# Hybrid diffusion layers on one core: in the first layer, tokens are normalised and transposed ahead of their modulation, which then goes by two blocks at a time

## The chip, the cores and the metric

The kernel runs on one NeuronCore of one Trainium2 chip. The metric is the device time of one execution in microseconds (us). Engines: TensorE (PE), VectorE (DVE), ScalarE (ACT), GpSimd (POOL), SyncE (SP, which here only issues DMAs).

## What is computed

Two layers over 512 latent and 256 context tokens of width 1024. Each layer starts with a normalisation whose result is scaled and shifted by columns computed from a condition vector; only this start matters here:

```python
shift, scale, gate = split(silu(c) @ w_mod[l] + b_mod[l], 3)      # c_ctx for context tokens
h = rmsnorm(x, norm_gain[l]) * (1 + scale) + shift
za, zb, zh, zf, zg = split(h @ w_in[l], SPLIT_IDX)                # projections of four mixers and gates
# four mixers, merged by gates sigmoid(h @ w_merge) and projected by w_out
x = x + gate * merge_branches(h, (ya, yb, yh, yf), zg, w_up[l], w_merge[l], w_out[l])
```

All is float32. Projections are done as three matmuls in a rounded format (high x high, high x low, low x high), so every operand is split into a high and a low part.

## The kernel before, in words

The kernel records its instructions in program order, and a planner of its own (`Program.order`, line 255) writes the final order of each engine, by assumed costs, ranks and free buffers. What runs on the chip is that fixed order: each engine takes its instructions one after another and waits by semaphores. SBUF tiles of 768 columns come from one pool of 31 slots (`slot`, line 371); PSUM has three 512-wide tiles (`psg`), two 1024-wide ones (`psw`) and one more (`pst`). All instructions are recorded through one helper, so every row of the profile has line 345, and rows are told apart by tiles.

Tokens are kept transposed, as features on partitions: `h_hi` and `h_lo` hold eight blocks of 128 features by 768 tokens (latent 0 to 511, context 512 to 767). A projection (`gemm_a`, line 583) goes through the eight blocks with 24 matmuls; `mm3` (line 572) lets the planner cut between groups of `ATOM` = 4 blocks. The first is `hg_gates` (line 1166): two outputs of 128 features, each over 384 and 384 tokens. Weights come by SP in pieces of 512 KB (`Weights`, line 484: tile `wraw`), and are split by ScalarE (`wh`) and VectorE (`wl`).

The opening of layer 0 is `first_modulation` (line 632) with `loads` (line 1503). Four loads of 2 MB of modulation weights (scale and shift of feature blocks 0 to 3, then of 4 to 7), each in eight DMAs, alternate with the x tokens, half of them after the first and half after the second. For each load, eight matmuls against the condition (`spread`, tile `cst`) give rows, ScalarE copies them, four small matmuls turn them into columns (`psg<-kc,mrow`). `Norm.square` (line 712) makes the sums of squares on ScalarE, `Norm.scale` (line 717) a reciprocal root in a chain of 13 small VectorE operations and a diagonal matrix from it; `Norm.place` (line 729) multiplies each token tile by that matrix, which transposes and normalises at once, scales and shifts on the way out of PSUM and splits. Half of the blocks is placed after two of the four loads, the other half at the end. `modulation` (line 662) does the same columns for layer 1 later, 256 at a time.

Of the kernel before, what the change touches and what calls it, by code (L numbers as in the profile page):

```python
# [21 lines left out]
P = 128  # L22
# [327 lines left out]
def tile_hybrid_mixers(ctx, tc, io, out, dump=None):  # L350
# [221 lines left out]
    def mm3(ps, pairs):  # L572
        n = len(pairs)
        nc.ahead = -BEHIND
        for k, (sh, sl, mh, ml) in enumerate(pairs):
            if k % ATOM == 0:
                nc.cut()
# [5 lines left out]
    def gemm_a(wh, wl, cs, n0, n1):  # L583
        ps = psg()[:, 0:n1 - n0]
        mm3(ps, [(wh[k][:, cs], wl[k][:, cs], hi_t[:, k, n0:n1], lo_t[:, k, n0:n1]) for k in range(8)])
        return ps
# [45 lines left out]
    def first_modulation(loads):  # L632
# [3 lines left out]
        for g in range(2):  # L636
            ks = slice(4 * g, 4 * g + 4)
            for a in (1, 0):
                nc.ahead = AHEAD
                w = []  # L640
                for k in range(8):
                    w.append(slot([P, 512]))
                    nc.sync.dma_start(w[k], io["w_mod0"][g, a, :, 512 * k:512 * (k + 1)])
                loads()
                ps = psg()
                for r in range(4):
                    nc.cut()
                    spread(ps, lambda k: w[k], (2 * r, 2 * r + 1))
                rows = sp.tile([P, 512], F32, tag="mth", bufs=2, name=nm("mrow"))
                act(rows, ps)  # L650
                pc = psg()[:, 0:8]
                for b in range(4):
                    mm(pc[:, 2 * b:2 * b + 2], rows[:, P * b:P * (b + 1)], csel)
                nc.ahead = 0
                bm = cols[:, CO_BM + 8 * a + 4 * g:CO_BM + 8 * a + 4 * g + 4]
                tt(tmp[:, a, ks], pc.rearrange("p (k w) -> p k w", w=2), bm.unsqueeze(2).to_broadcast([P, 4, 2]), ALU.add)
            ng = cols[:, CO_NG + 4 * g:CO_NG + 4 * g + 4]
            stt(mc[:, 0, ks], tmp[:, 1, ks], 1.0, ng.unsqueeze(2).to_broadcast([P, 4, 2]), ALU.add, ALU.mult)
            nc.vector.tensor_copy(mc[:, 1, ks], tmp[:, 0, ks])
            yield mc  # L660

    def modulation(l):
# [4 lines left out]
        def columns(j, rows):  # L667
            ps = psg()[:, 0:4]
            for b in range(2):
                mm(ps[:, 2 * b:2 * b + 2], rows[:, P * b:P * (b + 1)], csel)  # L670
# [3 lines left out]
        for j in range(8):  # L674
            rows = mod_rows(fetched.pop(("mod", j)))
            unit_done(2.0)
            if last is not None:
                columns(*last)
# [1022 lines left out]
```

## Time and profile before

| | us |
|---|---|
| median of 3 runs (1528.56 to 1533.97) | 1529.69 |
| the profiled execution | 1535.81 |
| its span in the profile | 1534.0 |
| TensorE busy | 1479.5 |
| VectorE busy | 941.7 |
| ScalarE busy | 633.8 |

The page shows one profiled execution: busy times, the span in 40 slices, DMA queues, the chain of work that ended last, and the costliest groups. The trace behind it can be asked for a stretch, an engine or a tile. A busy TensorE is not one at its peak: matmuls overlap, so the spacing of their starts says more than the length of one. [...]

### The profile page before, as it was taken

What the parts mean: (1) busy time and instruction counts of PE and PEld (TensorE: products, weight loads), DVE (VectorE), ACT (ScalarE), POOL (GpSimd) and SP (SyncE); (2) the same over time, 40 slices, a digit from 0 to 9 for tenths busy, and PEclk for the clock granted to TensorE, in tenths of its full rate; (3) what the DMA queues carried; (4) which work ended last, traced back from release to release, by engine and by line L of the source; (5) the groups of instructions that cost most, each with busy time, mean ns of one, the idle gap of its engine ahead of it and who ended that gap; (6) DMA issues with size and microseconds to landing.
All of it is one profiled execution on the core that took longest, in us unless ns stands there. A gap on an engine that the chain in (4) does not pass through costs nothing.

```text
span 1534.0 us, 25450 instructions
## 1 busy us (share of the span) xinstructions
PE 1479.5 (96%) x10052; PEld 1345.8 (88%) x10052; DVE 941.7 (61%) x2048; ACT 633.8 (41%) x1416; POOL 107.3 (7%) x207
## 2 busy tenths in 40 slices
PE   6899999999999998899999999999999999999999
PEld 2799989889999998889999998898987889888788
DVE  3596788667663355552444467978966864674544
ACT  3534354466532243441322244445445643552321
POOL 0000000410000000100000110000041000110000
PEclk8999999999999999899999999999999999999999
DMA  9211001523321124253221422111153222445332
GB/s 344 82 56 56 32 29 56 121 62 96 124 86 56 56 76 133 61 190 103 77 85 62 125 98 75 57 45 55 50 151 99 87 81 71 129 127 187 110 109 74
DMA packets 50280, 144.76 MB, mean 94 GB/s; under 512 B 7473, under 2 KB 9521, under 8 KB 50161
## 3 DMA queue, kind: packets, MB, share of 16 engines
q1 hardware_dynamic: 38016, 112.21, 22.5%
q0 software_dynamic: 12144, 30.93, 8.0%
q8 instruction: 79, 1.29, 0.3%
q14 instruction: 41, 0.33, 0.1%
HBM read 123.98 MB, written 4.19 MB: 84 GB/s over the span
## 4 chain that ended last, share of the span: by engine, by line
PE 85%; DVE 5%; ACT 5%; issue 2%; DMA 2%; SPq 0%; POOL 0%; ACTq 0%; DVEq 0%; POOLq 0%
PE psg L345 71%; PE psw L345 10%; PE pst L345 4%; ACT u L345 3%; DVE u L345 3%; DVE sm L345 1%; ACT wh L345 1%; DMA u<-in_w_mod_dram 1%; DVE wl L345 1%; DMA u<-u 0%; ACT mth L345 0%; DMA u<-in_rpb_dram 0%; SPq L345 0%; DVE psw L345 0%; ACT sq L345 0%
## 5 line engine op out<-in xcount | busy, mean ns | idle before, releaser
L345 PE MATMUL psg<-h_hi,wh 128*128 128x384 f32 (+2 forms) x1248 | 450.7, 361 | 5.4 <-ACT mth L345 2.8
L345 PE MATMUL psg<-h_lo,wh 128*128 128x384 f32 (+2 forms) x1248 | 440.6, 353 | 0.2 <-DVE h_lo L345 0.2
L345 PE MATMUL psg<-h_hi,wl 128*128 128x384 f32 (+2 forms) x1248 | 440.2, 353 | 0.0
L345 DVE TENSOR_TENSOR wl<-wraw,wh 128x512 fp32r<-128x512 f32 x312 | 201.6, 687 | 179.2 <-ACT wh L345 178.8
L345 ACT ACTIVATE wh<-wraw 128x512 fp32r<-128x512 f32 x312 | 180.5, 625 | 243.7 <-PE psg L345 226.7
L345 PEld LDWEIGHTS psg<-h_hi,wh 128*128 128x128 f32 x1248 | 236.5, 190 | 27.0 <-ACT mth L345 5.7
L345 PEld LDWEIGHTS psg<-h_hi,wl 128*128 128x128 f32 x1248 | 236.2, 189 | 15.8
L345 PEld LDWEIGHTS psg<-h_lo,wh 128*128 128x128 f32 x1248 | 236.9, 190 | 14.4 <-DVE h_lo L345 0.5
L345 PE MATMUL psw<-u,u 64*128 64x128 f32 (+5 forms) x1240 | 156.9, 301 | 19.8 <-ACT u L345 9.8
L345 PEld LDWEIGHTS psw<-u,u 64*128 64x128 f32 (+2 forms) x1240 | 127.2, 195 | 41.8 <-ACT u L345 21.0
L345 PE MATMUL psg<-wh,h_hi 128*128 128x256 f32 x544 | 159.0, 292 | 0.0
L345 PE MATMUL psg<-wl,h_hi 128*128 128x256 f32 x544 | 153.8, 283 | 0.0
L345 PE MATMUL psg<-wh,h_lo 128*128 128x256 f32 x544 | 153.7, 282 | 0.0
L345 ACT ACTIVATE u<-psw 128x768 f32<-128x768 f32 (+11 forms) x240 | 108.0, 475 | 71.7 <-PE psw L345 64.2
L345 ACT ACTIVATE u<-psw,sm 128x768 f32<-128x768 f32 (+2 forms) x120 | 90.6, 758 | 90.4 <-DVE sm L345 79.6
L345 ACT ACTIVATE mth<-psg 128x384 f32<-128x384 f32 (+1 forms) x120 | 62.1, 519 | 130.0 <-PE psg L345 127.4
L345 PE MATMUL psg<-wh,u 128*128 128x256 f32 x640 | 114.8, 281 | 0.9 <-ACT mth L345 0.9
L345 DVE SCALAR_TENSOR_TENSOR mth<-mth,psg 128x384 f32<-128x384 f32 (+1 forms) x96 | 57.1, 595 | 92.5 <-ACT mth L345 75.4
L345 PE MATMUL psg<-u,wh 128*128 128x384 f32 (+1 forms) x384 | 107.3, 360 | 0.8 <-DVE u L345 0.8
L345 PEld LDWEIGHTS psg<-wh,h_hi 128*128 128x128 f32 x544 | 104.0, 191 | 4.0
L345 DVE TENSOR_REDUCE sm<-psw 128x1 f32<-128x768 f32 (+3 forms) x100 | 89.6, 901 | 26.6 <-PE psw L345 25.9
L345 POOL DMA_DIRECT2D u<-u x132 | 65.2, 504 | 581.5 <-ACT u L345 369.0
(120 smaller groups left out, 1941.1 us busy)
## 6 DMA issues: line engine op xcount, KB each, us to landing
wraw<-in_w_merge_dram SPq DMA_DIRECT2D x64, 512.0 KB, 3.6
wraw<-in_w_in_dram SPq DMA_DIRECT2D x60, 512.0 KB, 3.8
u<-in_w_mod_dram SPq DMA_DIRECT2D x40, 256.0 KB, 5.4
wraw<-in_w_up_dram SPq DMA_DIRECT2D x16, 512.0 KB, 3.5
wraw<-in_w_out_dram SPq DMA_DIRECT2D x16, 512.0 KB, 4.0
u<-u POOLq DMA_DIRECT2D x72, 96.0 KB, 2.5
u<-in_w_mod_dram SPq DMA_DIRECT2D x16, 384.0 KB, 3.9
u<-in_w_gate_dram SPq DMA_DIRECT2D x16, 384.0 KB, 6.2
```

Source lines behind the costliest of these rows:

```text
L345: getattr(getattr(nc, engine), method)(*map(f, args), **{k: f(v) for k, v in kw.items()})
```

## The change

The four large loads and `first_modulation` go; `opening` takes their place. x comes in eight DMAs of 384 KB (three token tiles by 256 features), then eight modulation rows of 256 columns, each in three DMAs, in pairs of scale and shift that serve two feature blocks. The first four weight pieces are asked for ahead of that. Squares are now whole activations followed by VectorE reductions, the reciprocal root multiplies x in place, and 48 TensorE transposes with eight ScalarE copies make `xT`, all recorded ahead of any modulation. Then, pair by pair, rows, columns, scale and shift (VectorE, twice per block: latent and context) and the split. The first projection accumulates in the wide PSUM tiles, and the first two may be cut every two blocks. Masks are loaded from `hg_mix`. `modulation` of layer 1 uses the same column functions.

```diff
-    def mm3(ps, pairs):
+    def mm3(ps, pairs, atom=ATOM):
         n = len(pairs)
         nc.ahead = -BEHIND
         for k, (sh, sl, mh, ml) in enumerate(pairs):
-            if k % ATOM == 0:
+            if k % atom == 0:
...
-    def gemm_a(wh, wl, cs, n0, n1):
-        ps = psg()[:, 0:n1 - n0]
-        mm3(ps, [(wh[k][:, cs], wl[k][:, cs], hi_t[:, k, n0:n1], lo_t[:, k, n0:n1]) for k in range(8)])
+    def gemm_a(wh, wl, cs, n0, n1, ps=None, atom=ATOM):
+        ps = (psg() if ps is None else ps)[:, 0:n1 - n0]
+        mm3(ps, [(wh[k][:, cs], wl[k][:, cs], hi_t[:, k, n0:n1], lo_t[:, k, n0:n1]) for k in range(8)], atom)
...
-    def first_modulation(loads):
+    def columns(tmp, j, rows):
+        ps = psg()[:, 0:4]
+        for b in range(2):
+            mm(ps[:, 2 * b:2 * b + 2], rows[:, P * b:P * (b + 1)], csel)
+        nc.vector.tensor_copy(tmp[:, j // 4, 2 * (j % 4):2 * (j % 4) + 2, :], ps.rearrange("p (k w) -> p k w", w=2))
+
+    def mod_columns(l, mc, tmp, k0, k1):
+
+        ks, n = slice(k0, k1), k1 - k0
+        bm = cols[:, CO_BM + 24 * l:CO_BM + 24 * l + 16].rearrange("p (a k) -> p a k", a=2)
+        tt(tmp[:, :, ks], tmp[:, :, ks], bm[:, :, ks].unsqueeze(3).to_broadcast([P, 2, n, 2]), ALU.add)
+        ng = cols[:, CO_NG + 8 * l + k0:CO_NG + 8 * l + k1]
+        stt(mc[:, 0, ks], tmp[:, 1, ks], 1.0, ng.unsqueeze(2).to_broadcast([P, n, 2]), ALU.add, ALU.mult)
+        nc.vector.tensor_copy(mc[:, 1, ks], tmp[:, 0, ks])
+
+    def opening():
+
 
         mc = cpool.tile([P, 2, 8, 2], F32, tag="modc", bufs=1, name=nm("modc"))
         tmp = small(32, "mt", 1).rearrange("p (a k w) -> p a k w", a=2, w=2)
-        for g in range(2):
-            ks = slice(4 * g, 4 * g + 4)
-            for a in (1, 0):
-                nc.ahead = AHEAD
-                w = []
-                for k in range(8):
-                    w.append(slot([P, 512]))
-                    nc.sync.dma_start(w[k], io["w_mod0"][g, a, :, 512 * k:512 * (k + 1)])
-                loads()
-                ps = psg()
-                for r in range(4):
-                    nc.cut()
-                    spread(ps, lambda k: w[k], (2 * r, 2 * r + 1))
-                rows = sp.tile([P, 512], F32, tag="mth", bufs=2, name=nm("mrow"))
-                act(rows, ps)
-                pc = psg()[:, 0:8]
-                for b in range(4):
-                    mm(pc[:, 2 * b:2 * b + 2], rows[:, P * b:P * (b + 1)], csel)
-                nc.ahead = 0
-                bm = cols[:, CO_BM + 8 * a + 4 * g:CO_BM + 8 * a + 4 * g + 4]
-                tt(tmp[:, a, ks], pc.rearrange("p (k w) -> p k w", w=2), bm.unsqueeze(2).to_broadcast([P, 4, 2]), ALU.add)
-            ng = cols[:, CO_NG + 4 * g:CO_NG + 4 * g + 4]
-            stt(mc[:, 0, ks], tmp[:, 1, ks], 1.0, ng.unsqueeze(2).to_broadcast([P, 4, 2]), ALU.add, ALU.mult)
-            nc.vector.tensor_copy(mc[:, 1, ks], tmp[:, 0, ks])
-            yield mc
+        norm = Norm(None)
+        x = {}
+        for u in range(2):
+            for j in range(4):
+                x[j, u] = slot([P, 3, 256])
+                nc.sync.dma_start(x[j, u], io["xin"][384 * u:384 * (u + 1), 256 * j:256 * (j + 1)].rearrange("(t p) d -> p t d", p=P))
+        fetch = lambda i: [mod_fetch(io["w_mod"][0, j]) for j in (4 + i, i)]
+        w = {0: fetch(0)}
+        weights.fetch()
+        for u in range(2):
+            for j in range(4):
+                sq = slot([P, 3, 256])
+                act(sq, x[j, u], AF.Square)
+                nc.vector.tensor_reduce(norm.ss[:, 3 * u:3 * u + 3, j], sq, AX.X, ALU.add)
+            r = norm.rstd(3 * u, 3 * u + 3, 4)
+            for j in range(4):
+                tt(x[j, u], x[j, u], r.unsqueeze(2).to_broadcast([P, 3, 256]), ALU.mult)
+        w[1] = fetch(1)
+        xT = []
+        for i in range(4):
+            for k in (2 * i, 2 * i + 1):
+                ps = psw()[:, 0:NT]
+                for t in range(6):
+                    transpose(ps[:, P * t:P * (t + 1)], x[i, t // 3][:, t % 3, P * (k % 2):P * (k % 2 + 1)])
+                xT.append(slot())
+                act(xT[k], ps)
+        for i in range(4):
+            for j, wj in zip((4 + i, i), w.pop(i)):
+                columns(tmp, j, mod_rows(wj))
+            mod_columns(0, mc, tmp, 2 * i, 2 * i + 2)
+            for k in (2 * i, 2 * i + 1):
+                for c, n0, n1 in ((0, 0, NX), (1, NX, NT)):
+                    ts(xT[k][:, n0:n1], xT[k][:, n0:n1], mc[:, 0, k, c:c + 1], mc[:, 1, k, c:c + 1])
+                split(hi_t[:, k, :], lo_t[:, k, :], xT[k])
+            if i < 2:
+                w[i + 2] = fetch(i + 2)
+                for _ in range(4):
+                    weights.pump()
...
-        def columns(j, rows):
...
+        columns(tmp, *last)
+        mod_columns(l, mc, tmp, 0, 8)
...
+        def rstd(self, t0, t1, n):
             v = small(3, "sv", 1)
             m = t1 - t0
             nc.vector.tensor_reduce(v[:, 0:m], self.ss[:, t0:t1, 0:n], AX.X, ALU.add)
             ts(v[:, 0:m], v[:, 0:m], 1.0 / D, EPS)
-            r = rsqrt(v[:, 0:m], m, 3)
+            return rsqrt(v[:, 0:m], m, 3)
...
+        first = l == 0 and j == 0
         for d in range(2):
-            for n0, n1 in a_ranges(True):
-                ps = gemm_a(wh, wl, slice(P * d, P * (d + 1)), n0, n1)
+            wide = psw() if first else None
+            for i, (n0, n1) in enumerate(a_ranges(True)):
+                ps = gemm_a(wh, wl, slice(P * d, P * (d + 1)), n0, n1, wide[:, 512 * i:512 * i + 512] if first else None, 2 if first else ATOM)
...
-                ps = gemm_a(wh, wl, slice(P * j, P * (j + 1)), n0, n1)
+                ps = gemm_a(wh, wl, slice(P * j, P * (j + 1)), n0, n1, None, 2 if l == 0 else ATOM)
...
+        if full:
+            load_masks()
...
-            norm = Norm(None)
-            pend, dgs = [], []
-
-            def loads():
-                for t in range(len(pend), min(len(pend) + 3, 6)):
-                    xt = [slot([P, 512]) for _ in range(2)]
-                    for i in range(2):
-                        nc.sync.dma_start(xt[i], io["xin"][P * t:P * (t + 1), 512 * i:512 * (i + 1)])
-                        norm.square(t, i, xt[i])
-                    pend.append([xt[i // 4][:, P * (i % 4):P * (i % 4 + 1)] for i in range(8)])
-                if len(dgs) < 2:
-                    dgs.append(norm.scale(len(pend) - 3, len(pend), 2))
-
-            for g, norm.mc in enumerate(first_modulation(loads)):
-                for t in range(6):
-                    norm.place(t, pend[t], dgs[t // 3][:, t % 3, :], (g,))
-            weights.fetch()
-            load_masks()
+            opening()
...
-    d["w_mod0"] = w_mod[0, :, :2 * D].reshape(8, P, 2, 2, 512).transpose(3, 2, 1, 0, 4).reshape(2, 2, P, 4096)
-    d["w_mod"] = blocks(w_mod[:, :, :2 * D], 8)[1:]
+    d["w_mod"] = blocks(w_mod[:, :, :2 * D], 8)
```


The order shows three places where this moves work. First TensorE. Before, in the third load's rows (`psg_308`), their columns (`psg_368`), placed token tiles (`psw`) and the first projection (`psg_394`):

```order
L345 MATMUL psg_308<-u_185,cst 32x512
L345 MATMUL psg_308<-u_189,cst 32x512
L345 MATMUL psw_358<-u_339,u_147 128x128 x4
L345 MATMUL psg_368<-kc,mrow_363 128x2 x4
L345 MATMUL psw_382<-u_339,u_153 128x128 x4
L345 MATMUL psg_394<-h_hi,wh_376 128x384
L345 MATMUL psg_394<-h_lo,wh_376 128x384
L345 MATMUL psg_394<-h_hi,wl_379 128x384
```

Now, the last two transposed groups (`kc,u`) followed by columns (`kc,mrow`) and rows (`u,cst`):

```order
L345 MATMUL psw_382<-kc,u_91 128x128 x3
L345 MATMUL psw_382<-kc,u_103 128x128 x3
L345 MATMUL psg_391<-kc,mrow_389 128x2 x2
L345 MATMUL psg_398<-u_149,cst 32x256 x3
L345 MATMUL psg_398<-u_151,cst 32x256 x3
L345 MATMUL psg_398<-u_154,cst 32x256 x2
L345 MATMUL psg_408<-u_158,cst 32x256 x3
L345 MATMUL psg_408<-u_160,cst 32x256 x3
L345 MATMUL psg_408<-u_165,cst 32x256 x2
L345 MATMUL psg_419<-kc,mrow_417 128x2 x2
L345 MATMUL psg_424<-kc,mrow_422 128x2 x2
```

Before, the first projection stands ahead of the last load's rows; now all 48 transposes stand ahead of the columns of the second pair (`psg_391` and `psg_419`), with the first row of the third pair (`psg_408`) between, and the first projection (`psw_491`) stands eleven rows further on, behind all eight modulation rows.

Second, ScalarE, where rows are copied (`mrow`) and blocks are split (`h_hi`). Before, around the third load's rows:

```order
L345 ACTIVATE h_hi<-u_352 128x4x128
L345 ACTIVATE mrow_363<-psg_308 128x512
L345 ACTIVATE u_366<-psw_358,modc_191 128x128 x2
L345 ACTIVATE wh_376<-wraw_197 128x512 x2
L345 ACTIVATE h_hi<-u_366 128x4x128
L345 ACTIVATE wh_388<-wraw_201 128x512 x2
L345 ACTIVATE u_409<-psw_382,modc_191 128x128 x2
L345 ACTIVATE h_hi<-u_409 128x4x128
```

Now, the rows of the third and fourth pair:

```order
L345 ACTIVATE mrow_417<-psg_398 128x256
L345 ACTIVATE mrow_422<-psg_408 128x256
L345 ACTIVATE h_hi<-u_318 128x768
L345 ACTIVATE h_hi<-u_344 128x768
L345 ACTIVATE mrow_459<-psg_433 128x256
L345 ACTIVATE mrow_465<-psg_450 128x256
L345 ACTIVATE h_hi<-u_356 128x768
L345 ACTIVATE h_hi<-u_368 128x768
L345 ACTIVATE mrow_498<-psg_474 128x256
L345 ACTIVATE h_hi<-u_380 128x768
L345 ACTIVATE h_hi<-u_394 128x768
```

Before, one copy of rows stands among splits of single token tiles; now the copies of the third pair's rows stand behind both splits of the second pair, and the last row's (`mrow_498`) behind both splits of the third.

Third, VectorE. Before, the end of the first reciprocal root, the diagonal matrix (`u_230`) and the first scaled tiles:

```order
L345 SCALAR_TENSOR_TENSOR sm_228<-sm_210,sm_224 128x3
L345 TENSOR_SCALAR u_230<-kc,sm_228 128x128 x3
L345 TENSOR_TENSOR sm_187<-psg_266,cols 128x8
L345 COPY modc_191<-sm_187 128x8
L345 TENSOR_SCALAR u_279<-psw_238,modc_191 128x128 x2
L345 TENSOR_SCALAR u_282<-psw_247,modc_191 128x128 x2
```

Now, the end of the second reciprocal root and what follows (`u_93` to `u_103` are the second half of x):

```order
L345 SCALAR_TENSOR_TENSOR sm_276<-sm_246,sm_261 128x3
L345 TENSOR_TENSOR u_93<-u_93,sm_276 128x768
L345 TENSOR_TENSOR u_97<-u_97,sm_276 128x768
L345 TENSOR_TENSOR u_99<-u_99,sm_276 128x768
L345 TENSOR_TENSOR u_103<-u_103,sm_276 128x768
L345 TENSOR_TENSOR wl_310<-wraw_143,wh_300 128x512 x2
L345 COPY sm_255<-psg_315 128x4
L345 TENSOR_TENSOR sm_255<-sm_255,cols 128x2x4
L345 SCALAR_TENSOR_TENSOR modc_331<-sm_255,cols 128x4
L345 COPY modc_331<-sm_255 128x4
L345 TENSOR_SCALAR u_298<-u_298,modc_331 128x512
L345 TENSOR_SCALAR u_298<-u_298,modc_331 128x256
```

Where a diagonal matrix of 128 columns was made, four multiplications of 768 columns and a weight split (`wl_310`) now stand ahead of the first pair's columns (`sm_255`, `modc_331`).

## Rows read from the trace of the kernel before

**Rows 1.** the page, sections 1 (busy time by engine) and 4 (the chain).

```profile
PE 1479.5 (96%) x10052; PEld 1345.8 (88%) x10052; DVE 941.7 (61%) x2048; ACT 633.8 (41%) x1416; POOL 107.3 (7%) x207
...
PE 85%; DVE 5%; ACT 5%; issue 2%; DMA 2%; SPq 0%; POOL 0%; ACTq 0%; DVEq 0%; POOLq 0%
```

**Rows 2.** three stretches; columns as the second row says.

```profile
core 0: us, PE busy (x) PEld busy (x) DVE busy (x) ACT busy (x) POOL busy (x), PEclk, DMA share, GB/s
0.00:20.00 20.00, 10.57 (x31) 2.75 (x32) 3.27 (x18) 5.88 (x15) 2.99 (x9) 0.90 0.91 309
20.00:40.00 20.00, 15.39 (x77) 8.70 (x72) 9.14 (x38) 8.97 (x24) 0.56 (x2) 0.76 0.95 355
...
80.00:100.00 20.00, 20.00 (x140) 19.61 (x140) 19.97 (x26) 7.29 (x14) 0.00 (x0) 1.00 0.29 96
```

**Rows 3.** the chain's pieces in order of time: start us, us, what, count.

```profile
45.63 3.72 PE psg L345 x20
...
50.44 4.30 PE psg L345 x20
...
57.34 3.81 PE psg L345 x12
...
65.98 24.12 PE psg L345 x139
```

**Rows 4.** timeline of ScalarE: start us, us, instruction [idle before <-releaser].

```profile
13.62 0.63 ACT L345 ACTIVATE sq<-u 128x512 f32<-128x512 f32 x1 [8.25 <-DMA u<-in_xin_dram]
...
23.11 0.63 ACT L345 ACTIVATE sq<-u 128x512 f32<-128x512 f32 x1 [4.53 <-DMA u<-in_xin_dram]
```

**Rows 5.** timeline of VectorE, same columns.

```profile
18.61 0.16 DVE L345 TENSOR_REDUCE sm<-nss 128x3 f32<-128x6 f32 x1 [2.28 <-ACT sq L345]
...
21.24 0.68 DVE L345 TENSOR_SCALAR u<-kc,sm 128x128 f32<-128x128 f32 x3
...
43.61 1.29 DVE L345 TENSOR_TENSOR wl<-wraw,wh 128x512 fp32r<-128x512 f32 x2
```

**Rows 6.** VectorE's groups by form: xcount | busy us, mean ns | idle before.

```profile
L345 DVE TENSOR_TENSOR u<-u,sm 128x768 f32<-128x768 f32 x17 | 15.9, 955 | 0.2
...
L345 DVE TENSOR_SCALAR u<-u,sm 128x512 f32<-128x512 f32 x32 | 14.3, 483 | 0.5
...
L345 DVE TENSOR_REDUCE sm<-u 128x12 f32<-128x768 f32 x12 | 11.4, 953 | 31.8 <-ACT u L345 31.7
...
L345 DVE TENSOR_SCALAR u<-u,sm 128x256 f32<-128x256 f32 x8 | 2.5, 350 | 0.2
```

**Rows 7.** ScalarE's groups by form, same columns.

```profile
L345 ACT ACTIVATE u<-psw 128x768 f32<-128x768 f32 x38 | 30.8, 811 | 15.3 <-PE psw L345 13.2 <-DVE u L345 1.6
...
L345 ACT ACTIVATE u<-u 128x768 f32<-128x768 f32 x29 | 24.5, 846 | 11.6 <-DVE u L345 11.1
```

**Rows 8.** TensorE: one group by form, then timeline pieces (psw<-kc,u are transposes).

```profile
L345 PE MATMUL psg<-u,cst 128*32 128x256 f32 x256 | 17.1, 385 | 0.0
...
26.13 1.05 PE L345 MATMUL psg<-kc,mrow 128*128 128x2 f32 x8 [0.85 <-ACT mrow L345]
...
598.96 1.04 PE L345 MATMUL psw<-kc,u 128*128 128x128 f32 x8
...
606.91 1.97 PE L345 MATMUL psw<-kc,u 128*128 128x128 f32 x8 [2.86 <-ACT u L345]
```

**Rows 9.** two stretches, columns as in rows 2, and TensorE's timeline there.

```profile
30.00:36.00 6.00, 5.42 (x19) 3.53 (x20) 4.25 (x18) 3.81 (x10) 0.00 (x0) 0.50 1.04 393
...
43.50:46.50 3.00, 2.94 (x12) 2.94 (x13) 2.90 (x6) 2.96 (x7) 0.32 (x1) 0.50 0.40 108
...
43.56 2.08 PE L345 MATMUL psw<-u,u 128*128 128x128 f32 x8 [0.89 <-DVE u L345]
```

**Rows 10.** TensorE's waits from 70 to 400 us.

```profile
engine line waited for: us in total, times, longest us
PE psw L345 <- ACT u L345: 7.2, 12, 1.1
```

More of the change, by code (lines that the diff above doesn't have):

```diff
@@ L665, in modulation @@
         tmp = small(32, "mt", 1).rearrange("p (a k w) -> p a k w", a=2, w=2)
-        def columns(j, rows):
-            ps = psg()[:, 0:4]
-            for b in range(2):
-                mm(ps[:, 2 * b:2 * b + 2], rows[:, P * b:P * (b + 1)], csel)
-            nc.vector.tensor_copy(tmp[:, j // 4, 2 * (j % 4):2 * (j % 4) + 2, :], ps.rearrange("p (k w) -> p k w", w=2))
         last = None
@@ L677, in modulation @@
             if last is not None:
-                columns(*last)
+                columns(tmp, *last)
             last = (j, rows)
             yield None
-        columns(*last)
-        bm = cols[:, CO_BM + 24 * l:CO_BM + 24 * l + 16].rearrange("p (a k) -> p a k", a=2)
-        tt(tmp, tmp, bm.unsqueeze(3).to_broadcast([P, 2, 8, 2]), ALU.add)
-        ng = cols[:, CO_NG + 8 * l:CO_NG + 8 * l + 8]
-        stt(mc[:, 0], tmp[:, 1], 1.0, ng.unsqueeze(2).to_broadcast([P, 8, 2]), ALU.add, ALU.mult)
-        nc.vector.tensor_copy(mc[:, 1], tmp[:, 0])
+        columns(tmp, *last)
+        mod_columns(l, mc, tmp, 0, 8)
         yield mc
@@ L715, in square @@
             act(junk, x, AF.Square, accum_out=self.ss[:, t, j:j + 1])
-        def scale(self, t0, t1, n):
+        def rstd(self, t0, t1, n):
             v = small(3, "sv", 1)
@@ L722, in scale @@
             ts(v[:, 0:m], v[:, 0:m], 1.0 / D, EPS)
-            r = rsqrt(v[:, 0:m], m, 3)
+            return rsqrt(v[:, 0:m], m, 3)
+        def scale(self, t0, t1, n):
+            m = t1 - t0
+            r = self.rstd(t0, t1, n)
             dg = slot([P, 3, P])
@@ L727, in scale, with place @@
             return dg
-        def place(self, t, x, dg, groups=(0, 1)):
+        def place(self, t, x, dg):
             w = 0 if t < 4 else 1
-            for g in groups:
+            for g in range(2):
                 ps = psw()[:, 0:512]
@@ L1537, in between @@
             for what, j in extra(l, n, db + 1):
-                fetched[what, j] = mod_fetch(io["w_gate"][l, j] if what == "gate" else io["w_mod"][0, j])
+                fetched[what, j] = mod_fetch(io["w_gate"][l, j] if what == "gate" else io["w_mod"][1, j])
             for what, j in extra(l, n, db):
```

## Prediction

> **What bounds the kernel now.** I began with the shares and the chain of the page [rows 1]: TensorE is busy 96% of the span and holds 85% of the chain that ended last, so a microsecond counts where TensorE would otherwise wait. The change touches the opening, so I next read the first stretches [rows 2]: until 40 us the DMA engines are full (309, then 355 GB/s), and TensorE has half-empty, half-clocked work. In the chain [rows 3] the reader should look for the point from which TensorE runs projections without a break: 65.98 us. Before it, three groups of 12 projection matmuls have slipped in (the pieces of 20 hold 8 others each). The unbroken piece does 139 matmuls in 24.12 us, 0.174 us each, so the 36 early ones were worth 6.3 us. **The projections therefore stand as if they had begun at 65.98 - 6.3 = 59.7 us.** The same figure for the changed kernel is what has to be found; the gain is the difference, if nothing later takes it back.
>
> **What is removed, added, moved.** The loads are the same x and modulation weights in larger pieces, with the first four weight pieces of w_in ahead of or among them. Removed: the diagonal scaling matmuls and the scaling on the way out of PSUM, 96 small operations. Added: eight squares, reductions and multiplications over 768 columns, 48 TensorE transposes, eight 768-wide copies, and per pair of blocks a scale-and-shift, a split and four small column operations. They replace each other at about equal work, so what counts is the order in which they wait for each other. I follow it link by link.
>
> *Loads.* The first square started at 13.62 us on the ninth load of the sync queue (2.36 MB into it), the seventh after it at 23.11 on the 23rd (6.03 MB) [rows 4]: 0.387 MB per us. On that line the fourth x piece (2.62 MB into the new queue) is usable at 14.3, the eighth (4.19 MB) at 18.4, the last modulation weights (13.63 MB, 36 loads) at 42.7. Pieces of x now have runs half as long; I take no loss for that and up to 2 us into the range.
>
> *Normalising, on VectorE.* From 14.3: a square of 0.85 [rows 7], a reduction of 0.95 [rows 6], then the chain of small operations to the reciprocal root, 2.6 us (18.61 to 21.24 in [rows 5]), with two more reductions and a mask cast queued inside it (2.0): 20.8. One reduction (0.87; back to back a 0.95 us operation costs about 0.09 less, as the pair of 1.29 in [rows 5] does) and four multiplications of 0.955 [rows 6]: 25.1. The last reduction, the second chain and a weight split of 1.29 queued inside it: 29.9. The first multiplication of the second half ends at 30.8, the last at 33.4. VectorE has no gap from 15 to 34, so later loads would hardly move this.
>
> *Transposing, on TensorE.* It has only 6 records to do before 30.8; 90 follow (a transpose is two). Eight records take 1.04 us at full clock, 1.97 at half [rows 8]; start to start that is 0.11 and 0.22. After such a wait the trace shows half clock for some 3 to 6 us (30 to 36, 43.5 to 46.5 in [rows 9]); I take 4.5. So 20 records in 4.5 us, 70 in 7.8, and inside them one modulation row (16 records, 17.1 us / 16 = 1.07 in [rows 8]) and half a microsecond for copies of 0.81 [rows 7] that share ScalarE with splits of 0.85: 44.6.
>
> *Columns.* The rows and columns of the second pair of blocks stand behind the transposes in TensorE's queue, and the row after them ahead of the columns: two modulation rows (2.1) and the column matmuls (0.5, half of the 1.05 in [rows 8]) later, at 47.5, VectorE has them. The weights for these rows (10.49 MB into the queue) were usable at 34.6, so **the loads no longer set the end**.
>
> *Pairs, on VectorE.* One pair costs a copy and three small operations (0.8), scale and shift of 512 and 256 columns twice (2 x (0.483 + 0.350) less overlap, 1.5) and two splits (ScalarE's 0.85, then 2 x 0.95 less overlap): 4.3 us. In ScalarE's queue the next modulation rows stand behind the two splits of the pair before, so the pairs are strictly in series: second ready at 52, third at 56, fourth at 60.4. The first was ready at 42.
>
> *Projections.* In TensorE's queue one block of six matmuls (1.04) stands ahead of the last columns, which wait for ScalarE's copy of the last row (behind the third pair's splits) until 55.5; then five more blocks stand ahead of the first that reads the fourth pair. Those run 55.9 to 61.1, so the fourth pair is just in time. The projections stand as if begun at 55.9 - 1.0 = 54.9. TensorE idles by gaps of about 1 us from 50 to 56, and after two such gaps [rows 9] it ran 3 us at half clock; the same again costs 1.5: **56.4**. Atoms of two instead of four blocks change the order, not the number of matmuls; nothing for that. Masks are loaded at the same place of GpSimd's queue as before: nothing.
>
> *Sum.* 59.7 - 56.4 = 3.3 us less. Later waits of TensorE are copies it would have anyway (7.2 us in 12 between 70 and 400 [rows 10]), which I leave as they are. The profiled execution took 1535.81 us and would become 1532.5; it lies 6.1 above the median of the runs, 1529.69, from which the same difference gives **1526.4**. Bounds: 2 us earlier in the x pieces, no half clock at all (2.2 + 1.5) gives a gain near 9; half clock throughout the transposes gives the loss below. I take the middle since the stretch is like 24 to 44 us of the trace, where both levels alternate.
>
> **Rivals.**
>
> *The loads set the end (faster).* If VectorE and ScalarE ran ahead more than I think, the last modulation row would follow its weights at 42.7 and the fourth pair be ready some 7 us on (1.1 + 0.4 + 0.5 + 4.3 and links), 49.5; with six blocks ahead of it the projections stand as begun at 43.5 to 45. Gain 15, 1514.7. For it: TensorE's queue would then have three pairs to work on while the last arrives. Against: the 33.4 us of normalising, and pairs in series. A half-way case (gain 8 to 11) needs VectorE's second chain 5 us earlier. Together 0.25.
>
> *Transposes never leave half clock (slower).* Place: 30.8 to 45, TensorE. In 606.91 to 609 eight transposes alone, after a wait for a copy, ran at 0.22 a record, and so could all 90 here, each group of twelve waiting for a copy: 70 more records at 0.11 extra are 7.7 us, and modulation rows after them at half clock 2 or 3 more. The projections would stand as begun at 65 to 67: a loss of 5 to 7.5 us, 1535 to 1537. It decides from about 50 of the 90 records at half clock on; there the gain is gone. Against: the same transposes ran at full clock at 598.96 [rows 8], though among matmuls. 0.18, a third of it slower by over 0.5%, as VectorE's work behind the first gates then starts late in a stretch where it is full (19.97 of 20 us at 80 to 100 [rows 2]). [...] The row at 598.96 shows transposes at full rate, but none shows a long run of them alone.
>
> *Gained and given back (no change).* The order of the next 300 us on TensorE is also different in places; a side branch that is placed earlier than its VectorE input can wait. 1529 to 1531. 0.12.
>
> *The change does not do what it says:* the loads of the last pairs wait in the sync queue for buffers. The buffers they take come free at 22 to 26 (first row done, reductions done), before the queue reaches those loads (about 34): under 0.03, counted with no change.
>
> **How the numbers follow.** Forecast 0.45 (gain 1 to 7), faster cases 0.25, half clock 0.18, no change 0.12. A measurement tells a difference of about 0.5%, 7.6 us, from none. Faster by more: 0.24. Slower by more: 0.08. The rest, 0.68, is within. The range leaves out the fastest and the slowest tenth: 1517 to 1536.5.
>
> **What would show it.** Right: no projection before 52 us, and an unbroken run from 55 to 57; the last modulation weights landed near 43, ten microseconds before the row that uses them; transposes from 31 to 45 with half clock at first; splits of pairs 4 us apart. Wrong: a modulation row that waits for its weights (then the first rival), or granted clock 0.5 from 31 to 50 (the second), or a start at 56 and the same end (the third).

## The result, and the profile after

The changed kernel took 1518.51 us (1517.29 to 1520.19) beside 1529.85 for the kernel before: ratio 0.9922, 95% interval 0.9901 to 0.9943, so 11.3 us faster (8.7 to 15.1). That is inside the range and on the forecast side, but more than three times the forecast 3.3 us, and it is the outcome "faster by more than 7.6 us" to which I had given 0.24. Two causes add up: one term of my sum was too large by 5 us, and one that the sum lacked came on top. The second is luck, as the last group of experiments shows.

The page of the changed kernel, sections 1 and 4 [rows 1]:

```profile
PE 1457.1 (96%) x10068; PEld 1331.9 (88%) x10068; DVE 953.6 (63%) x2058; ACT 628.5 (41%) x1384; POOL 106.7 (7%) x207
...
PE 85%; DVE 6%; ACT 5%; issue 2%; DMA 1%; SPq 0%; ACTq 0%; DVEq 0%; POOLq 0%
```

The shares say nothing has changed, the sums do: TensorE is idle 61.3 us (1518.4 - 1457.1) where it was 54.5, and busy 22.4 us less. A change that was to let it wait less made it wait more and work less. The extra idle time is all in the opening: behind 66 us before and behind 51 us now, where the unbroken runs have begun, it is 36.6 and 36.7 us (length of the stretch less PE busy). Before, then now, columns as in [rows 2] (PEclk is the clock that TensorE was granted, as a share of the full one):

```profile
66.00:1534.00 1468.00, 1431.37 (x9824) 1315.97 (x9823) 914.61 (x1959) 603.49 (x1347) 101.58 (x193) 0.99 0.29 87
```

```profile
51.00:1518.40 1467.40, 1430.72 (x9854) 1313.84 (x9853) 916.15 (x1963) 602.49 (x1344) 101.09 (x193) 0.99 0.29 88
```

The first stretches, same columns:

```profile
0.00:20.00 20.00, 0.58 (x6) 0.22 (x6) 11.68 (x33) 10.43 (x14) 2.98 (x9) 1.00 0.95 306
20.00:40.00 20.00, 15.85 (x116) 10.87 (x114) 17.49 (x40) 10.55 (x17) 2.27 (x5) 0.91 1.04 399
...
80.00:100.00 20.00, 20.00 (x192) 18.51 (x192) 18.76 (x33) 10.18 (x21) 0.00 (x0) 1.00 0.16 53
```

TensorE is almost empty until 20 us, VectorE is what is full, and the loads now run at 399 GB/s. ScalarE's timeline of the fourth and the last square [rows 4]:

```profile
13.80 0.84 ACT L345 ACTIVATE u<-u 128x768 f32<-128x768 f32 x1 [0.28 <-DMA u<-in_xin_dram]
...
18.38 0.84 ACT L345 ACTIVATE u<-u 128x768 f32<-128x768 f32 x1 [0.29 <-DMA u<-in_xin_dram]
```

VectorE's timeline: the second set of multiplications, the two columns of the second pair, and the splits of pairs two to four:

```profile
28.71 3.56 DVE L345 TENSOR_TENSOR u<-u,sm 128x768 f32<-128x768 f32 x4
...
39.76 0.16 DVE L345 COPY sm<-psg 128x4 f32<-128x4 f32 x1 [1.25 <-PE psg L345]
42.16 0.16 DVE L345 COPY sm<-psg 128x4 f32<-128x4 f32 x1 [2.24 <-PE psg L345]
...
44.61 1.83 DVE L345 TENSOR_TENSOR h_lo<-u,h_hi 128x768 fp32r<-128x768 f32 x2
...
48.81 1.83 DVE L345 TENSOR_TENSOR h_lo<-u,h_hi 128x768 fp32r<-128x768 f32 x2
...
53.38 1.83 DVE L345 TENSOR_TENSOR h_lo<-u,h_hi 128x768 fp32r<-128x768 f32 x2
```

TensorE's timeline, transposes (`kc,u`), the first projection, the last columns, and the first matmul of the unbroken run:

```profile
29.72 3.05 PE L345 MATMUL psw<-kc,u 128*128 128x128 f32 x15 [2.79 <-DVE u L345]
...
33.28 1.66 PE L345 MATMUL psw<-kc,u 128*128 128x128 f32 x12
...
38.50 0.88 PE L345 MATMUL psw<-kc,u 128*128 128x128 f32 x6
...
48.01 0.69 PE L345 MATMUL psw<-h_hi,wh 128*128 128x384 f32 x1
...
50.09 0.78 PE L345 MATMUL psg<-kc,mrow 128*128 128x2 f32 x4
50.74 0.42 PE L345 MATMUL psw<-h_hi,wh 128*128 128x384 f32 x1
```

Six projection matmuls have gone ahead of 50.74, so the projections stand as begun at 50.74 - 6 x 0.174 = 49.7 us, where the kernel before had 59.7 and I had forecast 56.4. **The row to stop at is the transposes: 3 + 15 + 12 + 6 + 6 + 6 = 48 records for 48 transposes.** I had counted two for each.

### The profile page after: what moved, and what is told of

Same layout as the page of the kernel before. It is cut to its first block, busy times and chain, and to the rows that moved or that the text cites. A ratio compares the mean times of both kernels' runs of the same rounds, so it can differ in the third digit from the quotient of the medians.

```text
span 1518.4 us, 25432 instructions
## 1 busy us (share of the span) xinstructions
PE 1457.1 (96%) x10068; PEld 1331.9 (88%) x10068; DVE 953.6 (63%) x2058; ACT 628.5 (41%) x1384; POOL 106.7 (7%) x207
## 4 chain that ended last, share of the span: by engine, by line
PE 85%; DVE 6%; ACT 5%; issue 2%; DMA 1%; SPq 0%; ACTq 0%; DVEq 0%; POOLq 0%
PE psg L345 69%; PE psw L345 11%; PE pst L345 4%; DVE u L345 3%; ACT u L345 3%; DVE sm L345 2%; ACT wh L345 1%; DMA u<-in_xin_dram 1%; ACT mth L345 0%; DVE wl L345 0%; DMA u<-in_rpb_dram 0%; DVE nss L345 0%; DVE psw L345 0%; SPq L345 0%; ACT h_hi L345 0%
## 5 line engine op out<-in xcount | busy, mean ns | idle before, releaser
L345 PE MATMUL psg<-h_hi,wh 128*128 128x384 f32 (+2 forms) x1216 | 439.6, 362 | 4.0 <-ACT mth L345 2.8
L345 PE MATMUL psg<-h_lo,wh 128*128 128x384 f32 (+2 forms) x1216 | 430.3, 354 | 0.2 <-DVE h_lo L345 0.2
L345 PE MATMUL psg<-h_hi,wl 128*128 128x384 f32 (+2 forms) x1216 | 430.4, 354 | 0.0
L345 PEld LDWEIGHTS psg<-h_hi,wh 128*128 128x128 f32 x1216 | 230.1, 189 | 24.9 <-ACT mth L345 5.7
L345 PEld LDWEIGHTS psg<-h_hi,wl 128*128 128x128 f32 x1216 | 229.8, 189 | 15.8
L345 PEld LDWEIGHTS psg<-h_lo,wh 128*128 128x128 f32 x1216 | 230.4, 189 | 14.8 <-DVE h_lo L345 0.5
L345 PE MATMUL psw<-u,u 64*128 64x128 f32 (+6 forms) x1144 | 141.2, 299 | 12.3 <-ACT u L345 7.5
L345 ACT ACTIVATE u<-psw 128x768 f32<-128x768 f32 (+12 forms) x248 | 114.4, 485 | 81.3 <-PE psw L345 72.7
L345 PEld LDWEIGHTS psw<-u,u 64*128 64x128 f32 (+2 forms) x1144 | 113.1, 192 | 28.3 <-ACT u L345 13.2
```

The lines of the kernel that those rows point to most:

```text
L345: getattr(getattr(nc, engine), method)(*map(f, args), **{k: f(v) for k, v in kw.items()})
```

## The experiments

The kernels ran in three groups, after_again to cut_of_four, x_first to all_four, and the rest, each with the kernel before beside it (medians 1532.3, 1534.4 and 1530.7 us); so ratios are compared, not times. "As begun" is the opening's figure, as above; where matmuls at half clock follow the start of the unbroken run, their extra time is added (in the changed kernel the projection matmuls from 48.49 to 50.09 us, at granted 0.50, start 0.32 us apart, and 0.17 apart behind 51.00, at 1.00).

**The changed kernel again.**

> The changed kernel once more, as the measure for the runs beside it. Ratio to the kernel before 0.990 to 0.994; projections as if begun at 49.5 to 50 us (the unbroken run's start less 0.174 us for each earlier projection matmul).

0.9906 (0.9890 to 0.9921), 1516.94 us; as begun at 50.4. One profiled execution of the same program thus differs from another by 0.7 us in the opening.

**Transposes as matmuls.** The one change that leaves the order of every engine as it was:

```diff
-                    transpose(ps[:, P * t:P * (t + 1)], x[i, t // 3][...])
+                    mm(ps[:, P * t:P * (t + 1)], x[i, t // 3][...], ident)
```

> The 48 transposes are made by ordinary fp32 matmuls against the identity, as the kernel before made its scaling; the order on every engine stays the same. Theory (my sum failed because it gave a transpose two records; the chain normalising, transposes, columns of the second pair, pairs sets the end): 96 records in place of 48, 45 more of them behind the second normalisation at about 0.133 us each, so the last one ends near 45 in place of 39.4 us, the second pair's columns reach VectorE near 47 to 48 in place of 42.2, the projections stand as begun at 54 to 56, and the time is 4.5 to 6.5 us above the changed kernel's. Rival (loads or VectorE set the end and the transposes lie beside them): within 1 us of the changed kernel.

0.9941 (0.9927 to 0.9956), 1523.50 us: 5.4 us above the changed kernel by the ratios, 6.6 by the medians. TensorE's timeline of this kernel:

```profile
29.59 6.28 PE L345 MATMUL psw<-kc,u 128*128 128x128 f32 x30 [2.01 <-DVE u L345]
...
36.07 5.60 PE L345 MATMUL psw<-kc,u 128*128 128x128 f32 x48
...
42.60 1.60 PE L345 MATMUL psw<-kc,u 128*128 128x128 f32 x12
...
55.58 0.67 PE L345 MATMUL psw<-h_hi,wh 128*128 128x384 f32 x1
```

96 records, the last ending at 44.2, which is the 44.6 of my prediction. Six projection matmuls stand ahead of 55.58 and ten at half clock, 0.32 us apart, follow it; the 37th starts at full clock:

```profile
62.48 0.34 PE L345 MATMUL psw<-h_hi,wh 128*128 128x384 f32 x1
```

That is as begun at 62.48 - 36 x 0.174 = 56.2, for the 56.4 of my prediction. So this kernel is the one I had costed, and the theory holds: the transposes are a link of the chain, and the second record was the 5 us. Yet it is still 9.0 us below the kernel before (0.9941), where the sum gave 3.3: with the opening as forecast, some 6 us of gain lie outside the opening.

**All modulation first.**

```diff
-            mod_columns(0, mc, tmp, 2 * i, 2 * i + 2)
-            for k in (2 * i, 2 * i + 1):
...
+        mod_columns(0, mc, tmp, 0, 8)
+        for k in range(8):
```

> All eight modulation rows and columns first, then one set of column operations, then scale, shift and split of all eight blocks: the pairs are undone, the early x and transposes stay. Theory (the gain is the early normalising and transposing; with cuts of two blocks the first gates can start on whatever blocks are ready): last columns near 49 us, first three blocks split near 54.5, all eight near 63.5 to 64; with four pieces of 1.04 us left then, the projections stand as begun at 51 to 53, the time is 1 to 4 us above the changed kernel's. Rival (the gain comes from pairs that are modulated as their columns arrive): as begun at 57 or later, 7 to 10 us above, so that nearly nothing of the gain is left.

0.9951 (0.9937 to 0.9966), 1524.87 us. TensorE's timeline:

```profile
50.50 0.69 PE L345 MATMUL psw<-h_hi,wh 128*128 128x384 f32 x1 [2.55 <-ACT h_hi L345]
52.06 0.69 PE L345 MATMUL psw<-h_lo,wh 128*128 128x384 f32 x1 [0.86 <-DVE h_lo L345]
```

From 52.06 it runs, twelve matmuls at half clock (some 1.7 us; the chain has 89 matmuls in 17.35 us from there, for 15.5 at 0.174 each): as begun near 53.6, 3 to 4 us later than with pairs, about as the theory had it. The time is 6.9 us above by the ratios, which was the rival's. The groups of 256-column matmuls are 2.1 us busier in this execution; the rest is open. Pairs are worth 3.5 us in the opening, up to 7 in time.

**Cuts of four blocks**, in the gates and in the query:

```diff
-            wide = psw() if first else None
...
-                ps = gemm_a(wh, wl, slice(P * d, P * (d + 1)), n0, n1, wide[...] if first else None, 2 if first else ATOM)
+                ps = gemm_a(wh, wl, slice(P * d, P * (d + 1)), n0, n1)
```

> The first gates and the query are again cut every four blocks and accumulate in the narrow PSUM tiles; the opening stays as changed. Theory (the chain up to the pairs sets the end): the first piece starts when the second pair is split, near 48 us, three first halves last to 55, the second halves wait under 1 us for the fourth pair: as begun at 50 to 51, the time 0 to 1.5 us above the changed kernel's. Rival (the finer cut carries a good part of the gain): 4 us above or more.

0.9912 (0.9895 to 0.9929), 1519.66 us; as begun at 52.67 - 12 x 0.174 = 50.6. Not to be told from the changed kernel: the finer cut carries nothing that these runs can see.

**x first.** The opening asks for the first weight pieces without their rank ahead:

```diff
-        weights.fetch()
+        weights.fetch(0)
...
-                nc.ahead = AHEAD
+                nc.ahead = ahead
                 nc.sync.dma_start(t, self.plan.pop(0))
```

> The changed kernel with the first weight pieces of w_in asked for behind x and the first pair's modulation weights instead of ahead of them (1.05 MB at 0.4 MB per us: x is there 2.6 us earlier), so VectorE's two splits of them move from ahead of the normalising into its second half. Theory (the chain from the normalising sets the end): second normalisation starts 2 to 2.6 us earlier, one split of 1.29 in it, first column of the second pair 1 to 2 us earlier, time 1 to 2 us below the changed kernel's. Rival (the modulation weights, all landed near 41 us as before, set the end): no difference, within 0.5 us.

1.0011 (1.0002 to 1.0021), 1535.81 us: neither theory, 14 to 16 us slower than the changed kernel. The edit did not bring what it was to bring. In the changed kernel two of the first four weight pieces (1.05 MB) stand ahead of x in the queue, the other two among the first modulation rows. Without them ahead the last x piece landed at 16.4 us for 18.3, but the last three squares wait for TensorE's first modulation row. ScalarE's timeline:

```profile
19.58 2.31 ACT L345 ACTIVATE u<-u 128x768 f32<-128x768 f32 x3 [5.60 <-PE psg L345]
```

The second set of multiplications starts at 30.2 in place of 28.7, so this run does not test its theory. (In the changed kernel the last modulation weights landed at 43.8 us, not near 41: the last of these loads starts at 35.3 and takes 8.5.) The opening explains little of the time. TensorE's timeline:

```profile
50.30 0.44 PE L345 MATMUL psw<-h_hi,wh 128*128 128x384 f32 x1
...
55.51 0.44 PE L345 MATMUL psw<-h_lo,wh 128*128 128x384 f32 x1 [0.59 <-DVE h_lo L345]
```

22 projection matmuls stand ahead of 55.51, so it stands as begun at 51.7, 1.3 us later than in after_again and 2.0 later than in the changed kernel's first profile. TensorE's idle time over the span is 63.5 us against 60.7 in after_again. What differs is its busy time, 1471.0 against 1454.0 us: the same matmuls each take longer, all through the program. That became the question of the last group.

**Columns ahead of transposes.**

```diff
+                nc.ahead = AHEAD
                 columns(tmp, j, mod_rows(wj))
+                nc.ahead = 0
```

> The changed kernel with modulation rows and columns ranked ahead of the transposes in TensorE's order, nothing else. Theory (VectorE waits 1.25 and 2.24 us between 38.4 and 42.2 for columns whose matmuls stand behind the last transposes): the second pair's columns reach VectorE near 38 to 39, pairs are split near 42.6, 46.8, 51.3; TensorE's own rows, transposes and columns end near 47; projections as begun at 47 to 48.5, time 1.5 to 3 us below the changed kernel's. Rival (TensorE's work in the opening, or the rows' weights, is what lasts): within 0.7 us.

0.9918 (0.9900 to 0.9936), 1520.49 us, not faster. TensorE's timeline:

```profile
45.33 1.54 PE L345 MATMUL psw<-kc,u 128*128 128x128 f32 x6
...
49.96 1.54 PE L345 MATMUL psw<-kc,u 128*128 128x128 f32 x6
...
51.97 0.85 PE L345 MATMUL psw<-kc,u 128*128 128x128 f32 x6
52.57 0.42 PE L345 MATMUL psw<-h_hi,wh 128*128 128x384 f32 x1
```

The planner put the last blocks' transposes behind the last rows; the last six start at 51.97, and the projections follow at once: as begun at 52.6, 2 to 3 us later. VectorE's wait for the second pair's columns fell from 3.5 to 2.0 us, and TensorE's own queue took its place.

**The same, and squares summed by ScalarE.**

```diff
-                sq = slot([P, 3, 256])
-                act(sq, x[j, u], AF.Square)
-                nc.vector.tensor_reduce(norm.ss[...], sq, AX.X, ALU.add)
+                for t in range(3):
+                    norm.square(3 * u + t, j, x[j, u][:, t, :])
```

> As the run before it, and the squares are summed by ScalarE itself (24 squares of 256 columns with a sum, in place of 8 of 768), so that VectorE loses its eight reductions of 0.95 us. Theory (normalising is the first link): the second normalisation starts 4 to 6 us earlier, near 23 to 25, transposes follow it, and then the rows wait for their modulation weights (landed near 41): as begun at 44 to 46, time 4 to 6 us below the changed kernel's. Rival (normalising is hidden once the columns are ranked ahead): the same as the run before it, within 0.7 us.

0.9888 (0.9870 to 0.9905), 1516.91 us. TensorE's timeline:

```profile
25.23 0.55 PE L345 MATMUL psw<-kc,u 128*128 128x128 f32 x3 [2.12 <-DVE u L345]
...
43.86 0.44 PE L345 MATMUL psw<-h_hi,wh 128*128 128x384 f32 x1
...
47.21 0.42 PE L345 MATMUL psw<-h_hi,wh 128*128 128x384 f32 x1
```

The transposes behind the second normalisation start 4.5 us earlier and the projections stand as begun at 47.21 - 1.0 = 46.2, 4.2 earlier than in after_again and 6.4 earlier than in rows_ahead, the run it differs from by the sums alone: normalising is the first link. It has the best ratio of all. By the ratios it is 2.8 us below after_again, for the 4 to 6 of the theory, and the two intervals overlap.

**All of these**, and the second block of each pair scaled by ScalarE:

```diff
+                    if k % 2:
+                        act(xT[k][:, n0:n1], xT[k][:, n0:n1], AF.Identity, scale=mc[:, 0, k, c:c + 1], bias=mc[:, 1, k, c:c + 1])
+                    else:
...
```

> The three edits before together (x ahead of w_in's pieces, columns ahead of transposes, sums by ScalarE) and the second block of each pair scaled and shifted by ScalarE, so that a pair takes VectorE 2.6 us in place of 4.3. Theory (the last modulation weights, landed near 41 us, are then the end): last row 42.2, columns 43.2, fourth pair split near 47, projections as begun at 43.5 to 45, time 5 to 6.5 us below the changed kernel's. Rival (something after the opening gives it back): the opening earlier by 5 and the time less than 2 us below.

0.9976 (0.9962 to 0.9989), 1530.04 us: 8 to 11 us slower than the changed kernel, although its opening is earlier. Twelve projection matmuls stand ahead of its unbroken run, which starts at 48.81, so as begun at 46.7; ten at half clock follow, which makes it some 48.3, 1.4 to 2.1 us earlier than the changed kernel. TensorE is busy 1473.1 us. It shares with x_first the place of the tiles that the last group is about.

**64 bytes.** In x_first the compiled program places `wh` and `wl` elsewhere: their addresses modulo 128 are 64, and 0 in the changed kernel. The last group moves `wh` and `wl`, or `h_hi` and `h_lo`, by 64 bytes with an unused tile of 16 floats, and leaves the order of TensorE, ScalarE and the loads alone. Of the four, the first alone ran beside the kernel that it alters; the other three are compared across groups, by their ratios. Two other small tiles are made smaller or shared where that is needed for the space or to move the rest back. In the kernel before:

```diff
+                    if g == 0 and t == 0:
+                        nc.vector.tensor_copy(cpool.tile([P, 16], F32, name="pad"), hi_t[:, 0, 0:16].bitcast(F32))
```

> The kernel before, with one unused tile of 64 bytes ahead of the split weights, so that wh and wl lie 64 bytes further on in each partition and nothing else moves (their addresses modulo 128 go from 64 to 0, which is what they are in the changed kernel); one small VectorE copy more. In steady runs at granted clock 1.00 a matmul of 256 columns comes every 119 ns in the kernel before (252 in 30 us from 526 us), every 112 to 118 in the changed one (267 and 254 in 30 us), every 118 in x_first. Theory (the place of the split weights sets the steady spacing, so part of the measured gain is not the opening's): 256-column matmuls 2 to 6 ns closer, time 4 to 10 us below the kernel before. Rival (spacing follows from something else, or from nothing that stays with a program): within 2 us of the kernel before.

1.0059 (1.0047 to 1.0072), 1539.33 us: a large effect, in the direction opposite to the one I gave.

In the changed kernel, a tile of 64 bytes moved from behind the weights to ahead of them, and the pad behind them:

```diff
-        th = small(16)
+        th = small(16, "th", 1)
+        nc.gpsimd.memset(th, 0.0)
...
+        nc.vector.tensor_copy(cpool.tile([P, 16], F32, name="pad"), xT[0][:, 0:16])
```

> The changed kernel with wh and wl 64 bytes further on (addresses modulo 128 from 0 to 64, as in the kernel before and in x_first), all other matmul operands where they were, same order on TensorE and ScalarE. Theory (place of the weights): steady spacing as in x_first or as in the kernel before, opening unchanged, time 6 to 20 us above the changed kernel's, so 1523 to 1537. Rival: within 2 us of it.

0.9978 (0.9969 to 0.9987), 1526.85 us: as expected, 9 to 11 us above the changed kernel.

In x_first the same tile was ahead of the weights already; made single, it moves them 64 bytes nearer, and the pad stands behind them:

```diff
-        th = small(16)
+        th = small(16, "th", 1)
...
+        nc.vector.tensor_copy(cpool.tile([P, 16], F32, name="pad"), xT[0][:, 0:16])
```

> x_first with wh and wl 64 bytes nearer (addresses modulo 128 from 64 to 0), h_hi, h_lo and the large tiles where they were, same order. Theory (x_first lost 17 to 19 us by the place of its weights and not by its order): 1516 to 1522. Rival (its order, or the place of the other tiles, cost it): 1533 to 1537.

0.9983 (0.9973 to 0.9993), 1528.19 us: between both; 4 us come back.

In ahead_accumulate the pad alone, behind the weights and ahead of `h_hi`:

```diff
+            if i == 0:
+                nc.vector.tensor_copy(cpool.tile([P, 16], F32, name="pad"), xT[0][:, 0:16])
```

> ahead_accumulate with h_hi and h_lo 64 bytes further on (addresses modulo 128 from 64 to 0), weights where they were. If only the weights' place counts: as ahead_accumulate, ratio to the kernel before 0.987 to 0.991. If the place of weights and inputs to each other counts: 6 us or more away from it. It is also the candidate for the fastest version, by its opening (projections as begun near 46 us, 4 earlier than in the changed kernel).

0.9968 (0.9955 to 0.9980), 1525.23 us: 12 us above ahead_accumulate, of which its opening explains 1 (as begun at 47.2). The weights were not moved, so what counts is where weights and inputs lie to each other.

The stretches of nothing but 256-column matmuls near 530 us, columns as in [rows 2]. The kernel before:

```profile
526.00:556.00 30.00, 30.00 (x252) 30.00 (x251) 11.20 (x23) 8.73 (x18) 0.00 (x0) 1.00 0.14 47
```

After_weights_64:

```profile
517.00:547.00 30.00, 30.00 (x253) 30.00 (x252) 11.55 (x24) 9.59 (x19) 0.00 (x0) 1.00 0.12 38
```

The changed kernel:

```profile
515.00:545.00 30.00, 30.00 (x267) 30.00 (x266) 12.48 (x25) 10.13 (x20) 0.00 (x0) 1.00 0.14 46
```

x_first:

```profile
519.00:549.00 30.00, 30.00 (x255) 30.00 (x254) 11.86 (x25) 9.74 (x19) 0.00 (x0) 1.00 0.12 40
```

Before_weights_64:

```profile
524.00:554.00 30.00, 30.00 (x267) 30.00 (x266) 11.42 (x24) 9.46 (x19) 0.00 (x0) 1.00 0.17 53
```

Granted clock 1.00 and no idle time in any of them, and yet 252 to 267 matmuls in 30 us. The same form later on, the kernel before and the changed one:

```profile
1270.00:1294.00 24.00, 24.00 (x202) 24.00 (x201) 8.93 (x21) 7.46 (x16) 0.00 (x0) 1.00 0.26 86
```

```profile
1256.00:1280.00 24.00, 24.00 (x214) 24.00 (x213) 9.96 (x25) 7.75 (x17) 0.00 (x0) 1.00 0.25 83
```

Stretches of 512 columns near 1400 us, the kernel before:

```profile
1409.00:1431.00 22.00, 22.00 (x99) 18.18 (x98) 10.60 (x17) 7.51 (x15) 0.00 (x0) 1.00 0.34 97
```

The changed kernel:

```profile
1393.00:1415.00 22.00, 22.00 (x98) 18.03 (x97) 10.41 (x17) 7.42 (x14) 0.00 (x0) 1.00 0.30 96
```

x_first:

```profile
1408.00:1430.00 22.00, 22.00 (x96) 17.71 (x95) 9.99 (x17) 7.49 (x14) 0.00 (x0) 1.00 0.32 96
```

All fourteen profiles, by the distance from `wh` to `h_hi` in bytes modulo 256 (the addresses are those of the built programs). The last two columns are the time from one start to the next in ns, the mean of 228 matmuls in a row between 1250 and 1300 us (256 columns) and of 96 in a row near 1400 us (512):

| distance | profiles | 256 columns, in 30 us near 530 | 256 columns, ns near 1270 | 512 columns, ns |
|---|---|---|---|---|
| 0 | before; after_weights_64 | 252; 253 | 120.0; 120.0 | 226.9; 227.1 |
| 64 | changed, twice; matmul_transposes, whole_modulation, cut_of_four, rows_ahead, ahead_accumulate | 267, 257; 257 in each | 113.4 in each | 228.9 in each |
| 128 | x_first; accumulate_inputs_64; all_four | 255; 255; 255 | 118.6; 118.7; 118.6 | 233.3 in each |
| 192 | before_weights_64; x_first_weights_64 | 267; 257 | 117.8; 117.8 | 233.4; 233.3 |

The distance sorts the last two columns without an exception; near 530 us the profiles at 64, and those at 192, show two spacings (267 and 257), the changed kernel both of them in two executions of one program. The matmuls of 256 columns that read `u` sort as well, by the distance from `wh` to `u`: 116.7 to 117.1 ns at 224 (nine profiles), 117.8 at 192 (one), 119.2 at 128 (one), 120.0 at 160 (three). Why the distance counts, and why there are two spacings near 530 us, is not settled. What is shown is that moving one operand by 64 bytes, with the order of TensorE and ScalarE unchanged and one small VectorE copy more, moves the time by 0.3 to 0.8%.

**How much of the gain is the opening's.** TensorE's groups by form (columns as in [rows 6]), one of each kind. The kernel before:

```profile
L345 PE MATMUL psg<-wh,h_hi 128*128 128x256 f32 x544 | 159.0, 292 | 0.0
...
L345 PE MATMUL psg<-wh,u 128*128 128x256 f32 x640 | 114.8, 281 | 0.9 <-ACT mth L345 0.9
```

The changed kernel:

```profile
L345 PE MATMUL psg<-wh,h_hi 128*128 128x256 f32 x544 | 156.3, 287 | 0.0
...
L345 PE MATMUL psg<-wh,u 128*128 128x256 f32 x640 | 114.2, 280 | 0.9 <-ACT mth L345 0.9
```

After_weights_64:

```profile
L345 PE MATMUL psg<-wh,h_hi 128*128 128x256 f32 x544 | 159.1, 293 | 0.0
...
L345 PE MATMUL psg<-wh,u 128*128 128x256 f32 x640 | 116.9, 283 | 0.9 <-ACT mth L345 0.9
```

Summed over the groups of 256 and 512 columns and those with `u`, the changed kernel is 6 us less busy than the kernel before at equal counts (8.3 less at 256 columns, 2.1 more at 512), after_weights_64 4 us more (all in those with `u`, whose distance also changed). The groups of 384 columns are left out, since the opening's half clock is in them. Taken out of the measured 11.3 less and 3.4 less (0.9978), this leaves 5 and 8 us; from after_again's 14.4 less, with its own sums, 9. So **the opening gave some 5 to 9 us, and the place of the tiles some 6**. This is an estimate from busy sums.

The spans of the profiled executions say the same in another way: 1534.0 - 1518.4 = 15.6 us less, of which 10.0 are ahead of the points as begun (59.7 and 49.7) and 5.6 behind them. For after_weights_64, where the distance is that of the kernel before, nothing is gained behind them: its span is 8.5 us shorter (1525.5) with an opening 9.6 us earlier (as begun at 50.1). The opening is 8.5 us earlier in place of 10.0 where the kernel before is taken from the profile of before_weights_64 (its unbroken run starts at 64.47, not 65.98). That the traces give more than the times (15.6 for 11.3, 8.5 for 3.4) stays open; the profiled execution of before, at 1535.81 us, was 6 and 5 us above the medians beside which these two kernels ran.

## Why the prediction was right and wrong

- *Loads*: right. 13.80 and 18.38 us for the 14.3 and 18.4 of the text, so the half-length runs cost nothing that shows there. The last modulation weights landed at 43.8 (42.5 in after_again) for 42.7, 2.8 us before the row that uses them (46.67) and not ten, since that row came early.
- *Normalising*: right, 1.1 us early. The first multiplication of the second half ends near 29.7 for 30.8.
- *Transposing*: **the step that failed, in the words "90 follow (a transpose is two)".** 45 followed, and they ended at 39.4, not 44.6. The term took 8 records of [rows 8] for four transposes; they were eight. My working with 45 records gives 44.6 - 4.9 = 39.7, the sum 3.3 + 4.9 = 8.2 us, and matmul_transposes, which has the 96, gives 5 to 6.6 us of it back. The half clock at the start was about right: TensorE was at granted 0.50 for 3.4 us here (below) and for 6.8 in after_again, where I took 4.5.
- *Columns and pairs*: the chain is as drawn, 5 us earlier: 42.16 for 47.5, pairs 4.2 to 4.6 us apart for 4.3, the last ready at 55.2 for 60.4. The wait of the last columns for ScalarE behind the third pair's splits is there.
- *Projections*: 49.7 for 56.4. 5 us of this are the chain. The rest is half clock: behind 50.74 the matmuls start 0.17 us apart, where in matmul_transposes, with the chain as I had it, ten behind 55.58 start 0.32 apart and cost the 1.5 that I had allowed.
- *"Equal work"*: wrong. The opening's transposes have half the records of the scaling matmuls they replace (48 for 96).
- *"If nothing later takes it back"*: the gap in the sum. It asked what later waits would do, and not whether the same matmuls keep their spacing. They came closer by accident of placement, some 6 us that nobody planned: that is luck, and the mechanism of the prediction has no part in it.
- *Rivals*: the loads did not set the end (the last rows were not waiting for weights), the transposes did not stay at half clock, nothing was given back. The faster side had 0.24, and it came by a way that was none of my cases. Of the signs that I named for "right", the half clock at first and the splits 4 us apart came; a first projection behind 52 us (48.0) and an unbroken run from 55 to 57 (50.7) did not.

## What to carry over

Count the records of an operation in the trace before pricing it, in a place where the code tells how many operations there are; a factor of two in one link of a chain was worth more than all other terms here. And when a change can move tiles, as x_first's did by asking for weights later, compare the steady spacing of a matmul form far from the change in both traces: if that has moved, the measured time is not the change's alone, and a 64-byte control run tells how much.

## What was not expected of the hardware

Steady matmuls in the rounded format (fp32r), at granted clock 1.00 with no idle time, changed their spacing by up to 6% with 64 bytes of distance between the two operands in the same partitions (252 against 267 in 30 us, before and before_weights_64). Near 1270 us it was 120.0 ns at a distance of 0 and 113.4 at 64. The sum of the prediction had no term for that.

The clock rose during transposes. The changed kernel's windows, columns as in [rows 2]:

```profile
31.00:32.00 1.00, 1.00 (x7) 0.92 (x6) 1.00 (x2) 1.00 (x3) 0.00 (x0) 0.50 1.04 390
...
33.00:34.00 1.00, 1.00 (x7) 1.00 (x8) 0.93 (x5) 0.62 (x1) 0.00 (x0) 0.70 1.04 400
34.00:40.00 6.00, 5.11 (x55) 3.79 (x57) 3.97 (x10) 5.32 (x8) 2.27 (x5) 1.00 1.04 398
```

From 30.2 to 33.6 us TensorE did transposes and four small matmuls at granted clock 0.50, then at 1.00 with more of the same. The starts of transposes lie 0.21 us apart in the first stretch and 0.11 in the second. In after_again the clock was 1.00 for the first nine transposes behind 29.77, 0.50 from 31.0 to 37.8, and 1.00 again, with transposes on both sides of each change. For cut_of_four and whole_modulation the same view shows 1.00 from the start, but their transposes too start 0.21 us apart until 35 us and 0.11 from there. Their traces hold no record of the clock before 35.05 and 35.21, and the view gives 1.00 where there is none: it should be checked against the spacing. In the changed kernel the 24 transposes from 33.28 to 37.5 us stand alone, and behind 33.6 they went at granted 1.00 (0.11 us apart): the rival in which they never leave half clock did not come.
